# Unsplit weight halves in the mixers' projections and entry chunks, and another room for the experts' sixth chunk

## The chip, the cores and the metric

The kernel runs on one core of a Trainium2 chip. The metric is the time of one launch in microseconds of device time; it was taken in three runs. PE is TensorE (matmuls), PEld its weight loads, DVE is VectorE, ACT is ScalarE, POOL is GpSimd, SP is SyncE, whose queue issues all the transfers here.

## What is computed

A decoder trunk of two layers on 256 tokens of width 1024, in float32. Each layer: RMSNorm, an input projection whose 2304 columns feed four token mixers (a Conformer convolution, a pooling mixer, a dilated attention, a differential attention), an output projection, a residual add; then RMSNorm and a channel mixer, which is a dense SwiGLU in layer 0 and a choice of two of eight SwiGLU experts in layer 1.

```python
for layer in range(DEPTH):
    h = rms_norm(x, norm1_g[layer])
    x = x + token_mixing(h, w_in[layer], ...)      # 9 groups of 256 columns in, 1024 out
    h = rms_norm(x, norm2_g[layer])
    if layer % 2 == 0:
        x = x + swiglu(h, ffn_w_gate[i], ffn_w_up[i], ffn_w_down[i])    # 2816 wide
    else:
        x = x + moe_swiglu(h, moe_router[i], moe_w_gate[i], moe_w_up[i], moe_w_down[i])  # 8 x 3584 wide
return rms_norm(x, final_g)
```

## The kernel before

All weights lie in memory as one stream of chunks, 128 partitions by 2048 float32 columns, 1 MB each: 13 for each mixer, 33 for the dense channel mixer, 42 for each expert. `chunk` loads one into the next buffer of a ring. Until the experts the ring is one pool of nine buffers (`RING`). Before the experts the ring is written anew: eight further buffers (`RING2`), each a pool of its own, take the room that the second mixer's tiles had, and stand in the order between the pool's first `RING - LATE` turns and its last `LATE`. With `LATE = 3` the experts' chunks take six buffers of the old pool, then the eight new ones, then three of the old pool. The DMA queue is in order: a load that waits for its buffer holds all that stand behind it.

Products keep float32 accuracy by a split. `halves` cuts a chunk into two halves of 1024 columns and each of them into a high part (a copy on ACT, rounded to the format fp32r, line 190) and a low part (chunk minus high part, on DVE, or on POOL for the halves named in `on_pool`, line 191). The four pools of high and low parts hold four halves (`HALVES`). The tokens are split in the same way into `hTh` and `hTl`. A product is then three fp32r matmuls: high by high, low by high, high by low (`moving` where the weights stream through the array, `still` where the tokens do; `products` issues them, line 219). Some small products (line 655, the scores, the 64-row experts) are single matmuls on unsplit float32.

A stage begins with `enter`: for each block of 128 tokens it adds the last products of the stage before to the residual x (`run`, `add`), normalizes (`normed`), turns the block with eight transposes (`turned`) and copies it out of PSUM as high and low parts (`evict_high` for block 0, whose low parts are put off, `evict_parts` for block 1). Then `first` multiplies the block with the stage's first chunk (`token_major`, 24 matmuls of 256 columns). The order on DVE and ACT is written out by hand there; `hold` makes the next four splits stand behind the last copies. There are three such entries: the first mixer, the dense channel mixer, the second mixer. The experts have one of their own, not touched.

In `mixer`, behind the entry and one chunk of the same kind (c0 + 1), three calls of `project` compute 512 columns each from two chunks (queries and keys of the differential attention, then values, then queries and keys of the dilated attention). A chunk has two halves, a half two blocks of 128 input rows, and each block is multiplied with both blocks of tokens: 12 matmuls of 512 columns a half. The second half's low part is made on POOL, but for one chunk of the six. Between the halves DVE is given three of the 62 taps of the convolution (`some_taps`, line 401), and the rotary embedding (lines 439 to 442), the score blocks (line 475) and the scaling of the probabilities (lines 530, 531) follow on DVE. The output projection (`out_proj`) comes last. Outside `enter` a planner orders each engine's instructions, by modelled times.

In the experts the first turn and four more have 64 rows and use unsplit float32; three have 128 rows and split their chunks.

Of the kernel before, what the change touches and what calls it, by code (L numbers as in the profile page):

```python
# [10 lines left out]
F32 = mybir.dt.float32  # L11
# [4 lines left out]
AF = mybir.ActivationFunctionType  # L16
# [25 lines left out]
BIG = 4096.0  # L42
RING = 9
RING2 = 8
LATE = 3
HALVES = 4
FIRST = 0
START = 12
ORDER = ((0, 1, 2), (0, 2, 1))
FILL = 6  # L50
BUSY = ((4, 6), (0, 2, 4, 6), 4, 3)
TAPS = 3
# [41 lines left out]
def trunk(ctx: ExitStack, tc: tile.TileContext, x_in, wst, cst, par_a, par_l, gains, out):  # L94
# [80 lines left out]
    gain0 = gain(0)  # L175
    nc.sync.dma_start(cs, cst)

    def halves(c, on_pool=(), between=lambda: None):

        r = chunk(c) if isinstance(c, int) else c  # L180
        res = []
        for j in range(2):
            w = r[:, j * 1024:(j + 1) * 1024]
            hi = hi_p.tile([P, 1024], F32R, name="hi")
            lo = lo_p.tile([P, 1024], F32R, name="lo")
            eng = nc.gpsimd if j in on_pool else nc.vector
            with ExitStack() as st:
                for ins in behind if split[0] >= FIRST else ():
                    st.enter_context(tc.issue_after(ins))
                nc.scalar.activation(hi, w, AF.Copy)  # L190
                eng.tensor_tensor(out=lo, in0=w, in1=hi.bitcast(F32), op=SUB)  # L191
            split[0] += 1
            if split[0] == HALVES:
                behind.clear()
            res.append((hi, lo))
            if j == 0:
                between()
        return res
# [8 lines left out]
    def moving(ps, xx, w):  # L207

        return (ps, xx[0], w[0]), (ps, xx[1], w[0]), (ps, xx[0], w[1])
# [5 lines left out]
    def products(items, start=False, stop=False):  # L215

        seq = [m for it in items for m in it]
        for n, (ps, lhs, rhs) in enumerate(seq):
            nc.tensor.matmul(ps, lhs, rhs, start=start and all(m[0] is not ps for m in seq[:n]),  # L219
                             stop=stop and all(m[0] is not ps for m in seq[n + 1:]))  # L220

    def cut(pair, *at):
        return tuple(w[at] for w in pair)

    def part(hi, lo, src, eng=nc.vector):
        a = nc.scalar.activation(hi, src, AF.Copy)
        return a, eng.tensor_tensor(out=lo, in0=src, in1=hi.bitcast(F32), op=SUB)
# [46 lines left out]
            w = tuple(h.rearrange("p (k c) -> p k c", k=4) for h in hs[j])  # L274
            products([still(ps, cut(w, ALL, k, col), cut(hTp, ALL, 4 * j + k)) for k in range(4)], j == 0, j == 1)

    def token_major(ps, hs, t, order):

        tt = slice(t * P, (t + 1) * P)
        for j in range(2):  # L280
            w = tuple(h.rearrange("p (k c) -> p k c", k=4) for h in hs[j])
            items = [moving(ps, cut(hTp, ALL, 4 * j + k, tt), cut(w, ALL, k)) for k in range(4)]
            products([[it[n] for it in items] for n in order], j == 0, j == 1)

    def turned_back(src):

        ps = tr.tile([P, NT, P], F32, name="tr")
# [20 lines left out]
    def enter(before, c, first):  # L308

        run, add, gb = before[:3] if before else (lambda t, some: None, lambda t: None, gain0)
        eng = mybir.EngineType
        lows = []

        def evict_high(ps, kk, tt):

            h = nc.scalar.activation(hTh[:, kk, tt], ps, AF.Copy)
            lows.append(lambda: nc.vector.tensor_tensor(out=hTl[:, kk, tt], in0=ps, in1=hTh[:, kk, tt].bitcast(F32), op=SUB))  # L320
            return h

        with tc.manual_schedule(engines={eng.Activation, eng.DVE} if before else {eng.Activation, eng.DVE, eng.PE}):
            run(0, range(4))
            add(0)
            normed(0, xs[:, 0], gb)
            if before:
                hs = halves(c, (1,))
                run(1, range(3))
                turned(0, evict_high)  # L330
                lows[0]()
            else:
                hs = halves(c, (0,), lambda: turned(0, evict_parts))
                busy(FILL)
            run(1, range(3, 4))
            add(1)
            for f in lows[1:]:
                f()
            normed(1, xs[:, 1], gb, eng=nc.scalar)
            first(0, hs)  # L340
            last = turned(1, evict_parts)
        hold(*last)
        first(1, hs)

    def mixer(layer, c0, before):
        lam_init = 0.8 - 0.6 * math.exp(-0.3 * layer)
        psA = []

        def first(t, hs):
            if t == 0:  # L350
                psA.append(acc.tile([P, NT, 2, P], F32, name="acc"))
            token_major(psA[0][:, t].rearrange("p a c -> p (a c)"), hs, t, ORDER[int(t > 0 or before is not None)])

        enter(before, c0, first)
        if before:
# [1 line left out]
        with ExitStack() as held:  # L357
# [51 lines left out]
            def project(c, hooks=()):  # L409

                hooks = iter(hooks)
                ps = [acc.tile([P, 512], F32, name="acc") for _ in range(NT)]
                for j in range(2):
                    hs = halves(c + j, () if c + j == c0 + 5 else (1,))
                    for q in range(2):
                        w = tuple(h.rearrange("p (k c) -> p k c", k=2) for h in hs[q])
                        products([moving(ps[t], cut(hTp, ALL, 4 * j + 2 * q + k, slice(t * P, (t + 1) * P)), cut(w, ALL, k))
                                  for k in range(2) for t in range(NT)], j + q == 0, j + q == 2)
                        for _ in range(2):
                            for f in next(hooks, ()):  # L420
                                f()
                            some_taps(TAPS)
                return ps
# [246 lines left out]
        gb = gain(2 * layer + 1)  # L670
        parts = [h for n in (2, 3) for h in halves(c0 + 9 + n, (1,))]
        if layer == 1:

            ring[:] = ring[:-LATE] + [ctx.enter_context(tc.tile_pool(name=f"raw{n}", bufs=1, reuse_waits="tile"))
                                      for n in range(RING2)] + ring[-LATE:]
            turn[0] = 0
        return *add_products([(cut(hTp, ALL, ORD[4 + n]), h) for n, h in enumerate(parts)], po), gb, held

    def dense_ffn(c0, before):
        ps0 = []  # L680

        def first(t, hs):
            if t == 0:
                ps0.append(sc.tile([P, NT, 2, P], F32, name="sc"))
            token_major(ps0[0][:, t].rearrange("p a c -> p (a c)"), hs, t, ORDER[1])

        enter(before, c0, first)
        held = ExitStack()
        wk = held.enter_context(tc.tile_pool(name="fw", bufs=2, reuse_waits="tile"))
        ng = NFB // 2  # L690
        po = []

        def down(g, parts):
            hs = halves(c0 + 3 * g + 2)
            for n, hp in enumerate(parts):
                products([moving(po[2 * t + hf], cut(hp, ALL, slice(t * P, (t + 1) * P)), cut(hs[n], ALL, cc))
                          for t in range(NT) for hf, cc in enumerate(HF)], g + n == 0)

        prev, last = [], []
        for g in range(ng):  # L700
            parts = []
            for n in range(2):
                if g + n == 0:
                    gate, up = (ps0[0][:, :, a] for a in range(2))
                else:
                    hs = halves(c0 + 3 * g + n)
                    ps = sc.tile([P, 2, S], F32, name="sc")
                    for ab in range(2):
                        channel_major(ps[:, ab], hs, ab)
                    gate, up = (ps[:, a].rearrange("p (t c) -> p t c", t=NT) for a in range(2))  # L710
                sg = wk.tile([P, NT, P], F32, name="sgf")
                nc.scalar.activation(sg, gate, AF.Silu)
                h = wk.tile([P, NT, P], F32, name="hf")
                nc.vector.tensor_mul(h, up, sg)
                hh = wk.tile([P, S], F32R, name="hh", bufs=4)
                hl = wk.tile([P, S], F32R, name="hl", bufs=4)
                parts.append((hh, hl))
                if g + n == 0:
                    h0 = h
                else:  # L720
                    part(hh, hl, h.rearrange("p t c -> p (t c)"))
                if g == 0 and n == 1:
                    part(*parts[0], turned_back(h0))
            if g == 1:
                po.extend(acc.tile([P, 512], F32, name="acc") for _ in range(4))
            if 0 < g < ng - 1:
                down(g - 1, prev)
            last = prev + parts
            prev = parts
        gb = gain(2)  # L730
        parts = [h for g in (ng - 2, ng - 1) for h in halves(c0 + 3 * g + 2)]
        return *add_products(list(zip(last, parts)), po), gb, held

    def moe(c0, before):
        with ExitStack() as st:
# [395 lines left out]
            with tc.If(most > S):  # L1131
# [5 lines left out]
                    nc.vector.tensor_sub(pos2[:, t], pos[:, t], off)  # L1137
                experts([Turn(MOE0 + e * ECH, pos2, comb, e, True) for e in range(NE)])

    done = mixer(0, 0, None)  # L1140
    done = dense_ffn(FFN0, done)
    done = mixer(1, L1_0, done)
# [130 lines left out]
```

## Time and profile before

| | us |
|---|---|
| median of 3 runs | 1259.69 |
| lowest and highest of them | 1259.45, 1261.0 |
| the profiled execution | 1259.51 |
| its span, first to last instruction | 1257.7 |
| busy in it: PE, DVE, ACT, POOL | 1196.7, 735.8, 591.5, 73.9 |
| moved by DMA | 421.98 MB |
| mean granted TensorE clock | 0.987 |

By stage, in us from the span's start: the first mixer to about 112, the dense channel mixer with its entry to about 303, the second mixer to about 421, the experts' routing to 436, the experts to 1243, the last norm to the end. A share of busy time is an average over stages with different limits, so the stages are read one by one.

### The profile page before, as it was taken

How to read it: one execution, taken by the hardware profiler on the slowest of the kernel's cores; microseconds unless marked ns; L12 is line 12 of the kernel's file. 1: busy time of each engine (PE TensorE's matmuls, PEld its weight loads, DVE VectorE, ACT ScalarE, POOL GpSimd, SP SyncE). 2: the span in 40 equal slices, each digit the busy share in tenths (PEclk: the TensorE clock that was granted, in tenths of full speed). 3: DMA queues.
4: the chain of work that ended last, by engine and by line, in shares of the span. 5: the costliest groups of instructions: out<-in, count | busy, mean ns of one | idle time of the engine just before them, and what ended most of it. 6: DMA issues, size and time to landing. Idle time of an engine off the chain costs nothing.

```text
span 1257.7 us, 16634 instructions
## 1 busy us (share of the span) xinstructions
PE 1196.7 (95%) x6154; PEld 790.3 (63%) x6154; DVE 735.8 (58%) x1118; ACT 591.5 (47%) x868; POOL 73.9 (6%) x45
## 2 busy tenths in 40 slices
PE   8789999999888999999999999999999999999975
PEld 6677899998767633588853368874338887333221
DVE  5996655556898521688861188883139887212112
ACT  5374544444556421577741277772137776122112
POOL 3313000000511100000000000000000000000000
PEclk8899999999999999999999999999999999999998
DMA  9532655554532999999999999999999999999995
GB/s 362 213 128 101 230 183 191 184 196 157 193 134 110 413 420 420 419 418 418 417 361 421 419 420 419 419 419 405 420 419 419 420 419 419 415 418 420 420 420 221
DMA packets 60139, 421.98 MB, mean 336 GB/s; under 512 B 6672, under 2 KB 6928, under 8 KB 10256
## 3 DMA queue, kind: packets, MB, share of 16 engines
q1 hardware_dynamic: 60048, 420.82, 83.0%
q8 instruction: 50, 0.82, 0.3%
q14 instruction: 41, 0.34, 0.1%
HBM read 419.75 MB, written 1.05 MB: 335 GB/s over the span
## 4 chain that ended last, share of the span: by engine, by line
PE 58%; DMA 6%; DVE 1%; ACT 1%; issue 0%; POOL 0%; POOLq 0%; ACTq 0%; SPq 0%; DVEq 0%
PE acc L219 19%; PE acc L1004 16%; PE sc L219 9%; PE sc L1051 8%; DMA raw<-wst 6%; PE tr L955 1%; PE tr L1022 1%; PE tr L1071 1%; PE tr L1028 1%; DVE lo L191 1%; PE tr L974 0%; PE tr L965 0%; ACT hi L190 0%; DVE x L1072 0%; DVE raw L915 0%
## 5 line engine op out<-in xcount | busy, mean ns | idle before, releaser
L191 DVE TENSOR_TENSOR lo<-raw,hi 128x1024 fp32r<-128x1024 f32 x351 | 419.9, 1239 | 114.7 <-ACT hi L190 109.9
L190 ACT ACTIVATE hi<-raw 128x1024 fp32r<-128x1024 f32 x370 | 374.0, 1054 | 134.6 <-PE acc L219 61.4
L1004 PE MATMUL acc<-raw,xt 128*64 128x512 f32 x1096 | 251.3, 597 | 5.9 <-DMA raw<-wst 5.6
L1014 DVE TENSOR_TENSOR xs<-xs,acc 64x512 f32<-64x512 f32 x70 | 48.3, 690 | 276.4 <-ACT xs L1013 276.3
L1013 ACT ACTIVATE xs<-acc 64x512 f32<-64x512 f32 x70 | 41.3, 590 | 272.5 <-PE acc L1004 272.5
L1004 PEld LDWEIGHTS acc<-raw,xt 128*64 128x64 f32 x1096 | 73.7, 136 | 150.0 <-issue 131.7
L219 PE MATMUL acc<-lo,xgh 128*128 128x512 f32 x336 | 134.4, 400 | 1.9 <-DVE lo L191 1.6
L219 PE MATMUL acc<-hi,xgh 128*128 128x512 f32 x336 | 132.8, 395 | 0.0
L219 PE MATMUL acc<-hi,xgl 128*128 128x512 f32 x336 | 132.8, 395 | 0.0
L1051 PE MATMUL sc<-raw,ht 128*64 128x512 f32 x552 | 126.3, 594 | 5.0 <-ACT xs L1013 2.6
L219 PE MATMUL sc<-hTh,hi 128*128 128x256 f32 x336 | 93.0, 277 | 0.0
L219 PE MATMUL sc<-hTl,hi 128*128 128x256 f32 x336 | 92.9, 277 | 0.0
L219 PE MATMUL sc<-hTh,lo 128*128 128x256 f32 x336 | 92.9, 276 | 0.0
L1051 PEld LDWEIGHTS sc<-raw,ht 128*64 128x64 f32 x552 | 39.2, 137 | 84.1 <-issue 77.3
L219 PE MATMUL acc<-lo,hTh 128*128 128x512 f32 (+1 forms) x192 | 69.2, 387 | 10.5 <-DVE lo L191 10.4
L219 PEld LDWEIGHTS acc<-lo,xgh 128*128 128x128 f32 x336 | 63.2, 188 | 21.3 <-DVE lo L191 6.4
L219 PEld LDWEIGHTS acc<-hi,xgl 128*128 128x128 f32 x336 | 63.2, 188 | 14.9
L219 PEld LDWEIGHTS acc<-hi,xgh 128*128 128x128 f32 x336 | 63.3, 188 | 14.1
L219 PE MATMUL acc<-hi,hTh 128*128 128x512 f32 (+1 forms) x192 | 70.5, 395 | 0.0
L219 PE MATMUL acc<-hi,hTl 128*128 128x512 f32 (+1 forms) x192 | 70.1, 385 | 0.2
L219 PE MATMUL sc<-hi,hmh 128*128 128x512 f32 x168 | 66.7, 397 | 0.0
L219 PE MATMUL sc<-hi,hml 128*128 128x512 f32 x168 | 66.3, 395 | 0.0
(273 smaller groups left out, 1557.4 us busy)
## 6 DMA issues: line engine op xcount, KB each, us to landing
raw<-wst SPq DMA_DIRECT2D x389, 1024.0 KB, 16.4
raw<-gains SPq DMA_DIRECT2D x4, 512.0 KB, 5.5
raw<-wst SPq DMA_DIRECT2D x4, 512.0 KB, 13.0
hi<-wst SPq DMA_DIRECT2D x4, 512.0 KB, 14.2
lo<-wst SPq DMA_DIRECT2D x4, 512.0 KB, 13.8
pl<-par_l SPq DMA_DIRECT2D x2, 803.5 KB, 9.2
out<-raw SPq DMA_DIRECT2D x4, 256.0 KB, 3.2
x<-x_in SPq DMA_DIRECT2D x2, 256.0 KB, 3.3
```

The source lines that it names most:

```text
L190: nc.scalar.activation(hi, w, AF.Copy)
L191: eng.tensor_tensor(out=lo, in0=w, in1=hi.bitcast(F32), op=SUB)
L219: nc.tensor.matmul(ps, lhs, rhs, start=start and all(m[0] is not ps for m in seq[:n]), stop=stop and all(m[0] is not ps for m in seq[n + 1:]))
L955: nc.tensor.matmul(pg[q].rearrange("p k c -> p (k c)"), OH[e][:, t], src[:, t, HF[q]], start=t + n == 0, stop=t + n == 2)
L1004: m = nc.tensor.matmul(ps[ROWS[k % 2]], XT[e][:, 4 * j + k], w[:, k % 2], start=j == 0 and k < 2, stop=j == 1 and k > 1)
L1013: nc.scalar.activation(dst[ROWS[0]], ps[ROWS[0]], AF.Copy)
L1014: nc.vector.tensor_add(dst[ROWS[0]], dst[ROWS[0]], ps[ROWS[1]])
L1022: nc.tensor.transpose(ps[:, n, :NARROW], hm[ROWS[0], n * P:(n + 1) * P], ident[ROWS[0], ROWS[0]])
L1028: nc.tensor.transpose(ps[:, n], hm[:, n * P:(n + 1) * P], ident)
L1051: m = nc.tensor.matmul(DP[e][hf][ROWS[n]], HT[i][:, 2 * j + n], half(r, n)[:, HF[hf]], start=s + j == 0, stop=s == NSLAB - 1 and j == 1)
L1071: nc.tensor.matmul(ps, OT[e][:, t], y, start=n == 0, stop=n == 1)
```

## The change

Three things are done at once.

In `project` the first half of each chunk is not split. `halves` gets an argument `whole`: halves named there are handed on as they are. Their product is one float32 matmul of the unsplit tokens with the unsplit half. The second half's low part is made on DVE in all six chunks; POOL has none of them any more.

In `enter` the first chunk is not split at all. The block of tokens is copied out of PSUM once more, unsplit, into a new tile `full` (8 KB a partition), and `products_of` multiplies it with the chunk, eight float32 matmuls of 256 columns in place of 24. Both blocks get the extra copy, on ACT, ahead of the high copy. The first block's two low copies are made after the second residual add. `token_major` goes.

`full` lives in a pool of its own, ahead of the mixers' tiles, and is closed before the experts' ring is made; one of the eight new buffers takes its room. With `LATE = 4` the experts' sixth chunk takes that buffer in place of one of the old pool, and a later one takes the old pool's.

```diff
-LATE = 3
+LATE = 4
@@ halves
-    def halves(c, on_pool=(), between=lambda: None):
+    def halves(c, on_pool=(), between=lambda: None, whole=()):
...
             w = r[:, j * 1024:(j + 1) * 1024]
+            if j in whole:
+                res.append((w,))
+                continue
             hi = hi_p.tile([P, 1024], F32R, name="hi")
@@ enter
         def evict_high(ps, kk, tt):
 
+            a = nc.scalar.activation(full[:, kk, tt], ps, AF.Copy)
             h = nc.scalar.activation(hTh[:, kk, tt], ps, AF.Copy)
             lows.append(lambda: nc.vector.tensor_tensor(out=hTl[:, kk, tt], in0=ps, in1=hTh[:, kk, tt].bitcast(F32), op=SUB))
-            return h
+            return a, h
+
+        def evict_all(ps, kk, tt):
+            a = nc.scalar.activation(full[:, kk, tt], ps, AF.Copy)
+            return a, *part(hTh[:, kk, tt], hTl[:, kk, tt], ps)
+
+        def products_of(t):
+            tt = slice(t * P, (t + 1) * P)
+            ps = first(t)
+            for k in range(KD):
+                nc.tensor.matmul(ps, full[:, k, tt], r[:, k * 256:(k + 1) * 256], start=k == 0, stop=k == KD - 1)
 
         with tc.manual_schedule(engines={eng.Activation, eng.DVE} if before else {eng.Activation, eng.DVE, eng.PE}):
             run(0, range(4))
             add(0)
             normed(0, xs[:, 0], gb)
+            r = chunk(c)
             if before:
-                hs = halves(c, (1,))
                 run(1, range(3))
                 turned(0, evict_high)
-                lows[0]()
             else:
-                hs = halves(c, (0,), lambda: turned(0, evict_parts))
+                turned(0, evict_all)
                 busy(FILL)
             run(1, range(3, 4))
             add(1)
-            for f in lows[1:]:
+            for f in lows:
                 f()
             normed(1, xs[:, 1], gb, eng=nc.scalar)
-            first(0, hs)
-            last = turned(1, evict_parts)
+            products_of(0)
+            last = turned(1, evict_all)
         hold(*last)
-        first(1, hs)
+        products_of(1)
@@ project
-                    hs = halves(c + j, () if c + j == c0 + 5 else (1,))
+                    hs = halves(c + j, whole=(0,))
                     for q in range(2):
                         w = tuple(h.rearrange("p (k c) -> p k c", k=2) for h in hs[q])
-                        products([moving(ps[t], cut(hTp, ALL, 4 * j + 2 * q + k, slice(t * P, (t + 1) * P)), cut(w, ALL, k))
-                                  for k in range(2) for t in range(NT)], j + q == 0, j + q == 2)
+                        at = [(4 * j + 2 * q + k, k, t, slice(t * P, (t + 1) * P)) for k in range(2) for t in range(NT)]
+                        if q == 0:
+                            products([[(ps[t], full[:, b, tt], w[0][:, k])] for b, k, t, tt in at], j == 0)
+                        else:
+                            products([moving(ps[t], cut(hTp, ALL, b, tt), cut(w, ALL, k)) for b, k, t, tt in at], False, j == 1)
@@ end of mixer, layer 1
+            full_only.close()
@@ before the stages
+    full_only = ExitStack()
+    full = full_only.enter_context(tc.tile_pool(name="hf", bufs=1, reuse_waits="tile")).tile([P, KD, S], F32, name="hTf")
```

## Rows read from the trace of the kernel before

**Rows 1.** The page, busy tenths and GB/s in 40 slices of 31.4 us.

```profile
DVE  5996655556898521688861188883139887212112
...
GB/s 362 213 128 101 230 183 191 184 196 157 193 134 110 413 420 420 419 418 418 417 361 421 419 420 419 419 419 405 420 419 419 420 419 419 415 418 420 420 420 221
```

**Rows 2.** Windows: us, busy (count) of PE, PEld, DVE, ACT, POOL; clock, DMA, GB/s.

```profile
26.00:52.00 26.00, 19.18 (x77) 15.34 (x76) 25.52 (x48) 8.35 (x11) 8.75 (x4) 0.80 0.74 296
42.00:52.00 10.00, 6.22 (x15) 4.87 (x16) 10.00 (x28) 1.06 (x1) 0.00 (x0) 0.50 0.36 120
52.00:78.00 26.00, 25.99 (x143) 20.49 (x141) 22.81 (x66) 17.78 (x42) 8.64 (x2) 1.00 0.41 148
...
326.00:349.00 23.00, 17.38 (x76) 13.52 (x75) 22.82 (x39) 9.23 (x12) 16.90 (x4) 1.00 0.32 115
349.00:385.00 36.00, 32.04 (x172) 25.82 (x172) 34.83 (x104) 20.36 (x49) 2.39 (x1) 0.91 0.39 147
```

**Rows 3.** Waits of PE, 26 to 112 us: total, times, longest.

```profile
PE acc L219 <- DVE lo L191: 6.8, 1, 6.8
```

**Rows 4.** Groups of DVE, 26 to 80 us: busy us, mean ns, idle before.

```profile
L401 DVE SCALAR_TENSOR_TENSOR cv<-zp,pl,cv 128x256 f32<-128x256 f32 x60 | 30.8, 581 | 0.0
L191 DVE TENSOR_TENSOR lo<-raw,hi 128x1024 fp32r<-128x1024 f32 x9 | 11.1, 1252 | 1.7 <-ACT hi L190 1.7
...
L475 DVE CUSTOM_DVE_ANT_0 pD<-sc,pl 128x128 f32<-128x128 f32 x8 | 1.9, 284 | 3.0 <-PE sc L469 3.0
```

**Rows 5.** Timeline of DVE, 326 to 350 us: start, us, instruction.

```profile
327.03 2.33 DVE L399 TENSOR_SCALAR cv<-zp,pl 128x256 f32<-128x256 f32 x1 [0.18 <-ACT zp L390]
...
338.26 1.21 DVE L191 TENSOR_TENSOR lo<-raw,hi 128x1024 fp32r<-128x1024 f32 x1
339.39 2.62 DVE L401 SCALAR_TENSOR_TENSOR cv<-zp,pl,cv 128x256 f32<-128x256 f32 x1
341.93 2.50 DVE L439 TENSOR_TENSOR xc<-xs,pl 128x128 f32<-128x128 f32 x1
...
344.56 0.47 DVE L401 SCALAR_TENSOR_TENSOR cv<-zp,pl,cv 128x256 f32<-128x256 f32 x1
...
345.62 0.28 DVE L439 TENSOR_TENSOR xc<-xs,pl 128x128 f32<-128x128 f32 x1
...
346.03 2.56 DVE L401 SCALAR_TENSOR_TENSOR cv<-zp,pl,cv 128x256 f32<-128x256 f32 x1
```

**Rows 6.** Timeline of POOL, 300 to 412 us.

```profile
345.62 2.69 POOL L191 TENSOR_TENSOR lo<-raw,hi 128x1024 fp32r<-128x1024 f32 x1 [1.33 <-ACT hi L190]
```

**Rows 7.** Chain of work that ended last: start, us, what, how many.

```profile
408.87 1.74 PE sc L655 x8
...
549.56 11.14 PE acc L219 x48
```

**Rows 8.** Timeline of ACT, 305 to 323 us.

```profile
316.54 1.26 ACT L226 ACTIVATE hTh<-tr 128x512 fp32r<-128x512 f32 x2 [2.48 <-PE tr L263]
317.70 2.95 ACT L190 ACTIVATE hi<-raw 128x1024 fp32r<-128x1024 f32 x3
```

**Rows 9.** Timeline of DVE, 305 to 327 us.

```profile
308.06 3.43 DVE L191 TENSOR_TENSOR lo<-raw,hi 128x1024 fp32r<-128x1024 f32 x1
...
318.78 3.50 DVE L191 TENSOR_TENSOR lo<-raw,hi 128x1024 fp32r<-128x1024 f32 x3 [0.25 <-ACT hi L190]
```

**Rows 10.** Waits of the DMA queue, 378 to 413 us.

```profile
SPq L159 <- DVE lo L191: 27.6, 2, 22.5
SPq L159 <- PE sc L666: 5.5, 1, 5.5
```

**Rows 11.** Windows in the experts, columns as in rows 2.

```profile
644.00:655.00 11.00, 11.00 (x49) 3.83 (x49) 4.91 (x7) 2.90 (x5) 0.00 (x0) 1.00 0.87 329
655.00:860.00 205.00, 203.50 (x924) 127.41 (x920) 127.31 (x134) 109.40 (x136) 0.00 (x0) 1.00 1.01 419
```

**Rows 12.** Waits of the DMA queue, 641 to 655 us.

```profile
SPq L159 <- PE acc L1004: 8.7, 4, 3.1
```

More of the change, by code (lines that the diff above doesn't have):

```diff
@@ L48 @@
 START = 12
-ORDER = ((0, 1, 2), (0, 2, 1))
 FILL = 6
@@ L275, in channel_major @@
             products([still(ps, cut(w, ALL, k, col), cut(hTp, ALL, 4 * j + k)) for k in range(4)], j == 0, j == 1)
[L277 to L283, printed above, removed]
     def turned_back(src):
@@ L347, in mixer, with first @@
         psA = []
-        def first(t, hs):
+        def first(t):
             if t == 0:
                 psA.append(acc.tile([P, NT, 2, P], F32, name="acc"))
-            token_major(psA[0][:, t].rearrange("p a c -> p (a c)"), hs, t, ORDER[int(t > 0 or before is not None)])
+            return psA[0][:, t].rearrange("p a c -> p (a c)")
         enter(before, c0, first)
@@ L680, in dense_ffn, with first @@
         ps0 = []
-        def first(t, hs):
+        def first(t):
             if t == 0:
                 ps0.append(sc.tile([P, NT, 2, P], F32, name="sc"))
-            token_major(ps0[0][:, t].rearrange("p a c -> p (a c)"), hs, t, ORDER[1])
+            return ps0[0][:, t].rearrange("p a c -> p (a c)")
         enter(before, c0, first)
```

## The prediction

> **What bounds the kernel now.** I read the slices of the page first [rows 1]. From about 400 us to the end the transfers run at 418 to 420 GB/s with two dents (361 and 405), so the experts stream their weights at the pace of memory. Before 400 us they run at 100 to 230 GB/s: memory has room there, and something on the core sets the time. The table by stage [rows 2] says what. In the two mixers' wide projections VectorE (DVE) is the fullest engine: 25.52 of 26.00 us in one stretch of mixer 0, 22.82 of 23.00 and 34.83 of 36.00 in mixer 1, while TensorE (PE) does 19.18, 17.38 and 32.04. The waits of PE [rows 3] agree: its longest wait in mixer 0, 6.8 us, is for a low half made by DVE, and behind it PE runs at a granted clock of 0.50 (1.2 of its two levels, 1.2 and 2.4 GHz) for ten us [rows 2]. Only 52 to 78 us is full on PE (25.99 of 26.00). So a saving on DVE in the mixers moves the start of the experts.
>
> Does an earlier start of the experts move the end? At 644 to 655 us the stream drops to 329 GB/s [rows 11] while the DMA queue waits 8.7 us for PE's reads of earlier chunks [rows 12]: all buffers were full and PE, in its first 128-row expert, was behind. PE's path from the start of the experts up to there is therefore on the chain, and behind it the stream runs full. If PE starts X earlier, that point comes X earlier and so does the end, as long as the stream is not the later one; it had 31.4 us x (1 - 361/419) = 4.4 us to spare in that slice [rows 1, 11], and its own start moves too (below). I pass X on whole.
>
> **Projections, DVE.** Each mixer has six wide chunks of two halves. Before, the first half's low part is made on DVE (1.21 us, [rows 5]) and, in five chunks of six, the second's on GpSimd (Pool). After, first halves have no low part and second halves' are made on DVE. So DVE loses six lows and gains five: -1.2 us a mixer. The larger part is what Pool does to DVE. While a Pool split runs (345.62 for 2.69 us, [rows 6]) a DVE tap that starts at 346.03 takes 2.56 us; alone it takes 0.47 [rows 5]. The same holds for 327.03 (2.33), 339.39 (2.62) and 341.93 (2.50 where the like operation takes 0.28). In mixer 1 that is (2.33 + 2.62 + 2.50 + 2.56) - (0.47 + 0.47 + 0.28 + 0.47) = 8.3 us, all under Pool splits that the change takes away. In mixer 0 the grouped rows give it: 60 taps of 581 ns where 470 is normal [rows 5], 6.6 us [rows 4]. The one Pool split of the output projection stays, with its 2 us. Mixer 0 also has 3.0 us in which DVE sat idle for score products that PE had not reached [rows 4], because PE had lost 6.8 us and then its clock; PE no longer waits for a low part in the first half of each chunk, and with one pair of buffers a chunk in place of two the splits can run two chunks further ahead. I count the 3.0 as gone. Sum: mixer 0 6.6 + 1.2 + 3.0 = 10.8, mixer 1 8.3 + 1.2 = 9.5.
>
> **Projections, PE.** A split product is three matmuls of 512 columns; 48 take 11.14 us [rows 7], 0.232 each, 0.70 a product. A 128x128 float32 matmul of 512 columns is not in this trace. The nearest row is line 655, float32, 128x128 weights, 256 columns: eight in 1.74 us [rows 7], 0.217 each, so I take 0.434 at 512. Bounds: 0.217 (as if the width cost nothing) and 0.70 (no gain). By 0.434 a half costs 4 x 0.434 = 1.74 in place of 2.79, -1.05, six times: -6.3 us of PE a mixer, which keeps PE ahead of DVE and is not added to the sum; at 0.70 PE would just stay where it is, and of the sum only the 3.0 idle would come back.
>
> Here a rule of the Trainium skill speaks against the change. "FP8 and Floating Point Precision", section TensorE Precision Notes, gives true FP32 four passes through the array. By it a 512-column product would take four times a one-pass 0.232, 0.93 against the 0.70 of the split one, and PE would gain work. Line 655's row is against it: 0.217 is about twice, not four times, what 256 columns take in one pass at half of 0.232.
>
> **Entries.** Three entries (mixer 0, dense FFN, mixer 1) follow one pattern. Removed: two high parts on ACT, a low part on DVE and one on Pool. At mixer 1 that DVE low takes 3.43 us [rows 9] since it collides with Pool's, and it stands ahead of the second residual add. Added: for each 128 tokens two plain ACT copies from PSUM. At the second block they stand between its two high copies (1.26 us for a pair, [rows 8]) and the next chunk's high parts (from 317.70, [rows 8]), whose low parts (from 318.78, [rows 9]) the next products need; the hold on the last evictions keeps that order, and ACT's queue behind it holds nothing but these. Cost +1.26 us each. Return: the add can start when PE's last products allow, about 1 us sooner, but the two held-back low copies now follow it ahead of the norm's scalar; I take, as an estimate, 1.0 back at FFN and mixer 1, and 0.1 at mixer 0, whose second block waits for its load. Together +1.2 + 0.3 + 0.3 = +1.8 us, bounds 0 to 3.8. The entry products themselves shrink from three matmuls to one of 0.217 and need ACT's copy alone, but the next chunk's split is late next, so I cost them at nothing; if ACT's order let the split go first, they would give up to 1 us each.
>
> **The sixth chunk.** Its DMA stands behind a wait of 22.5 of the 27.6 us for a split of the output projection [rows 10], in an idle memory stretch, and the queue is in order, so all later ones stand behind it. With the room of the unsplit tokens (last read in the third projection) it and the next few can go some 20 us sooner. But the stream then meets the next wait, for the last attention product (5.5 us, [rows 10]), which isn't moved: the chunks already taken are 2.5 us each (1 MB at 419 GB/s, [rows 11]), and between them and that wait the queue idles again; I estimate that one chunk's 2.5 us is left of it. That makes the stream earlier, not PE, so at 644 us the buffers are full again a little sooner: 0. Without this edit, the room would cost nothing either.
>
> **Sum.** 10.8 + 9.5 - 1.8 = 18.5 us. DVE is an in-order queue and won't be full all the time: PE, now with less work, waits longer before the last score blocks, and a wait of 6.8 us cost it ten us at half clock with 6.22 busy, 3.1 lost [rows 2, 3]. I charge 1.75 a mixer: -15. The profiled execution took 1259.5 (span 1257.7, 1.8 around it), the median of the runs is 1259.7: forecast 1245.
>
> **The rivals.**
> 1. DVE's queue gives bubbles: taps are queued ahead of the lows that PE needs, as is the case now at PE's wait of 6.8 us [rows 3], so only half of the saved time shows. For it: the order is made from modelled times and PE waits on DVE in other places too. Against: two fewer buffers per chunk. -4 to -10, 1253.
> 2. Slower: the six extra copies on ACT at the entries lie on the path and the mixers return nothing, because DVE's freed time is only waited out. Price 3 x 1.26 = 3.8, 1263. It decides once the mixers give back less than 1.9 us each; the 8.3 us of measured stalls speak against it.
> 3. The stream takes it: if loads of experts cannot start sooner, everything before is only waiting; 1257 to 1261. Against: every room they wait for is freed by mixer 1 itself.
> 4. A float32 matmul of 512 columns takes four passes of 0.232 [rows 7], 0.93: per mixer 24 x (0.93 - 0.70) = +5.5 us on PE in place of -6.3. PE then needs as long as DVE, the 3.0 idle stays and by estimate 2 us a mixer are lost to PE: 18.5 - 3.5 - 3.0 - 4 = 8, 1252. This is the skill's rule, above; line 655 is against it.
> 5. All of it comes, with the experts' early loads and no clock loss: -18 to -22, 1239.
>
> **Chances.** Forecast (-10 to -18) 0.56, rival 1 0.20, rival 2 0.06, rival 3 0.06, rival 4 0.04, rival 5 0.08. Bounds of the unknown costs (entries 0 to 3.8, idle 3.0, clock 0 to 6) keep the forecast within 1241 to 1250; the range for 8 in 10 takes in most of rivals 1, 4 and 5: 1238 to 1255. A measurement tells about 0.2% (2.5 us). Faster 0.88, within 0.06, slower 0.06.
>
> **What would show it.** After: Pool has no split between the entry and the output projection; no tap in the mixers over 0.5 us but one; mixer 1's projections end some 10 us sooner relative to its entry; float32 matmuls of 512 columns 0.43 apart; ACT with four copies in a row at each entry's second block; the dent at 640 us still there, a little deeper. The forecast is wrong if DVE in the mixers stands idle by more than 5 us each, if PE's clock is at 0.50 for over 15 us there, or if the dent vanishes and the stream runs at 419 GB/s from its start.

## The result, and the profile after

The changed kernel takes 1246.8 us (median of four runs, 1244.4 to 1250.7) against 1260.35 beside it: a ratio of 0.9899, 95% interval 0.9876 to 0.9922. The forecast was 1245, range 1238 to 1255. The total came as forecast; two of its steps have the wrong sign (PE's price for a float32 product, and the entries), and the runs below show what stood in for them.

The profiled execution is one of 1248.1 us. Its page, engines and slices, the counterpart of [rows 1]:

```profile
PE 1203.4 (97%) x6058; PEld 781.3 (63%) x6058; DVE 709.4 (57%) x1113; ACT 578.1 (46%) x862; POOL 30.7 (2%) x32
...
DVE  4975655555985512888841298883148886212112
...
GB/s 363 245 102 102 238 203 190 168 200 165 184 203 172 411 419 420 419 419 420 395 373 419 419 419 420 419 420 404 419 420 418 420 419 417 417 419 419 419 420 208
```

DVE's busy time fell by 26.4 us and Pool's by 43.2. The experts start 12.3 us earlier (first gather at 419.7 us, before at 432.0), and the dent in the stream spreads over two slices (395 and 373 GB/s, where one had 361). The windows are the counterpart of [rows 2], with the same columns:

```profile
26.00:52.00 26.00, 26.00 (x101) 16.59 (x101) 24.69 (x62) 7.67 (x11) 0.00 (x0) 1.00 0.74 294
52.00:78.00 26.00, 25.35 (x143) 17.75 (x143) 22.11 (x77) 16.40 (x45) 2.40 (x1) 1.00 0.57 203
82.70:92.90 10.20, 10.06 (x41) 8.78 (x41) 7.09 (x31) 5.01 (x16) 2.08 (x2) 0.50 0.00 0
...
322.00:349.00 27.00, 27.00 (x92) 16.48 (x91) 27.00 (x71) 8.43 (x11) 0.00 (x0) 1.00 0.37 137
349.00:385.00 36.00, 31.96 (x194) 23.41 (x193) 29.84 (x115) 21.67 (x66) 4.48 (x3) 1.00 0.62 230
```

From 26 to 52 us PE was busy 19.18 us; now it is busy 26.00, and in mixer 0 DVE is the one with time to spare. In mixer 1 (322 to 349 us) both are full, 27.00 of 27; e9 and e10 below tell which of them sets the time. The half clock at 42 to 52 us is gone, and another has come at 82.7, in the mixer's tail. PE's waits from 26 to 112 us, for [rows 3]:

```profile
PE sc L476 <- DVE nm L482: 1.6, 1, 1.6
PE tr L458 <- DVE xs L449: 0.7, 1, 0.7
```

No wait of PE for a low part is left. DVE's groups, 26 to 80 us, for [rows 4] (the last column is DVE's idle time before them and what ended it):

```profile
L405 DVE SCALAR_TENSOR_TENSOR cv<-zp,pl,cv 128x256 f32<-128x256 f32 x60 | 24.6, 480 | 0.0
L193 DVE TENSOR_TENSOR lo<-raw,hi 128x1024 fp32r<-128x1024 f32 x10 | 12.1, 1223 | 0.5 <-ACT hi L192 0.5
L482 DVE CUSTOM_DVE_ANT_0 pD<-sc,pl 128x256 f32<-128x256 f32 x8 | 3.0, 418 | 1.9 <-PE sc L476 1.9
L446 DVE TENSOR_TENSOR xc<-xs,pl 128x128 f32<-128x128 f32 x4 | 2.7, 686 | 1.6 <-ACT xs L438 1.6
```

The 60 taps fell from 30.8 to 24.6 us, 480 ns each in place of 581. And PE's groups from 26 to 70 us, the costliest:

```profile
L221 PE MATMUL acc<-raw,hTf 128*128 128x512 f32 x48 | 21.7, 594 | 0.0
L221 PE MATMUL acc<-hi,hTh 128*128 128x512 f32 x24 | 11.2, 467 | 0.0
L221 PE MATMUL acc<-lo,hTh 128*128 128x512 f32 x24 | 9.4, 394 | 0.0
L221 PE MATMUL acc<-hi,hTl 128*128 128x512 f32 x24 | 9.4, 391 | 0.0
```

This is the row that the prediction had wrong. The code issues four products per half, 24 in the six unsplit halves and 24 in the six split ones. The split ones show 24 rows for each of their three matmuls; the unsplit ones show 48. **A float32 matmul leaves two rows.** On the timeline of PE:

```profile
28.09 3.60 PE L221 MATMUL acc<-raw,hTf 128*128 128x512 f32 x8
...
34.29 3.60 PE L221 MATMUL acc<-raw,hTf 128*128 128x512 f32 x8
```

Eight rows for four products, 3.60 us from the first start to the last end, with the last row's own 0.594 in it: the starts are 0.429 us apart ((3.60 - 0.594) / 7). So a float32 product of 512 columns takes 0.858 us, more than the three split matmuls (0.70).

### The profile page after: what moved, and what is told of

It reads as the page before. It is cut to its first block, busy times and chain, and to the rows that moved or that the text cites. A ratio compares the mean times of both kernels' runs of the same rounds, so it can differ in the third digit from the quotient of the medians.

```text
span 1246.1 us, 16416 instructions
## 1 busy us (share of the span) xinstructions
PE 1203.4 (97%) x6058; PEld 781.3 (63%) x6058; DVE 709.4 (57%) x1113; ACT 578.1 (46%) x862; POOL 30.7 (2%) x32
## 4 chain that ended last, share of the span: by engine, by line
PE 52%; DMA 14%; DVE 1%; ACT 1%; issue 0%; POOL 0%; POOLq 0%; SPq 0%; ACTq 0%; DVEq 0%
PE acc L221 19%; DMA raw<-wst 14%; PE acc L1012 13%; PE sc L221 9%; PE sc L1059 6%; PE tr L963 1%; PE tr L1036 1%; PE tr L1079 1%; PE tr L1030 1%; DVE lo L193 1%; ACT hi L192 0%; DVE x L1080 0%; PE tr L973 0%; DVE raw L923 0%; PE tr L982 0%
## 5 line engine op out<-in xcount | busy, mean ns | idle before, releaser
L193 DVE TENSOR_TENSOR lo<-raw,hi 128x1024 fp32r<-128x1024 f32 x346 | 406.9, 1220 | 115.8 <-ACT hi L192 112.7
L192 ACT ACTIVATE hi<-raw 128x1024 fp32r<-128x1024 f32 x352 | 355.0, 1055 | 109.3 <-PE acc L221 48.5
L221 PEld LDWEIGHTS sc<-hTl,hi 128*128 128x128 f32 x336 | 63.2, 188 | 0.4
L221 PEld LDWEIGHTS sc<-hTh,hi 128*128 128x128 f32 x336 | 63.1, 188 | 0.4
L221 PEld LDWEIGHTS sc<-hTh,lo 128*128 128x128 f32 x336 | 63.1, 188 | 0.0
```

## Experiments

To place a saving I cut each profiled execution at the same events: the first tap of a mixer, the last scaling of the first attention's weights (between them lie the wide projections), the last attention product, the first gather of the experts, and the end. In us, from the timelines (each time is that of the profiled execution, one per kernel):

| kernel | first tap to scaling, mixer 0 / 1 | from there to the last attention product, 0 / 1 | gather to end |
|---|---|---|---|
| before | 57.2 / 57.6 | 27.7 / 28.3 | 825.7 |
| after | 50.9 / 49.2 | 30.6 / 28.4 | 826.4 |
| e1, five early | 50.9 / 49.2 | 29.7 / 28.4 | 826.3 |
| e2, entries alone | 58.7 / 57.7 | 28.8 / 29.6 | 827.0 |
| e3, FFN's entry split | 50.9 / 49.2 | 30.6 / 30.3 | 827.4 |
| e4, lows on Pool | 56.0 / 54.3 | 29.6 / 30.4 | 825.8 |
| e5, before, lows on DVE | 54.4 / 53.2 | 29.4 / 27.4 | 826.2 |
| e9, fewer taps | 50.9 / 49.2 | 29.6 / 28.4 | 826.0 |
| e10, half the products | 46.9 / 44.6 | 30.0 / 29.3 | 826.2 |
| e11, all split on DVE | 54.8 / 51.6 | 29.3 / 28.9 | 826.7 |
| e12, three unsplit | 49.2 / 47.9 | 27.7 / 27.7 | 825.6 |

**e1: the sixth early chunk undone.**

```diff
-LATE = 4
+LATE = 3
```

> The changed kernel with the sixth early chunk undone (five loads of the experts before mixer 1 ends, as before the change), all else kept. Theory (the prediction's step): the stream of the experts starts about one chunk, 2.5 us, later, but at about 640 us all buffers are full and PE's path decides, so the time stays that of the changed kernel, 1246.8 within 1.5 us; the dent in the stream at 600 to 660 us gets smaller by about 2.5 us of stream. Rival (the earlier chunk counts in full, the stream decides): 1249.3. Rival (the room costs, and undoing it gains): under 1245.

Measured: 1248.2 (1245.7 to 1249.5), ratio 0.9901 (0.9886 to 0.9916); after has 0.9899. No difference, as the theory has it. The last column of the table says why: from the first gather to the end it is 826.3 against 826.4, whichever stream started first. The dent's windows, first e1, then after:

```profile
600.00:660.00 60.00, 59.91 (x275) 33.80 (x275) 33.22 (x38) 25.72 (x35) 0.00 (x0) 1.00 0.96 384
```

```profile
600.00:660.00 60.00, 59.91 (x274) 34.90 (x274) 33.93 (x38) 26.32 (x36) 0.00 (x0) 1.00 0.96 382
```

384 against 382 GB/s is 60 x 2/419 = 0.3 us of stream, not the 2.5 expected of the dent. That the chunk is worth nothing is shown; that the dent swallows it is not.

**e2: the unsplit entries alone** (`project` as before the change).

```diff
-                    hs = halves(c + j, whole=(0,))
+                    hs = halves(c + j, () if c + j == c0 + 5 else (1,))
...
```

> The changed kernel with the mixers' wide projections split as before the change (both halves, the second's low part on Pool), the unsplit entries and the sixth chunk kept. Theory as the two traces now suggest: the entries gained about 3 us (FFN 2, mixer 1 one), so the projections carry 10: 1257 (1255 to 1258.5). The prediction's own terms: the entries lose 1.8, so 1262. Rival (the entries carry most): 1250 or less.

Measured: 1259.9 (1258.9 to 1262.8), ratio 0.9996 (0.9988 to 1.0005): outside the theory's range, between the two. The way from mixer 0's last attention product to mixer 1's first tap, with two entries in it, is 211.4 us against 213.8 before, so they did bring 2.3. The mixers of the profiled run, the slowest of the twelve (1262.8), are 1.5 and 0.2 longer up to the scaling and 1.1 and 1.3 behind it, with the clock at half in six short stretches of them (before has three). In the total, the entries alone are worth nothing that can be measured.

**e3: the dense FFN's entry alone as before** (`enter_split` is the former `enter`, with `token_major`).

```diff
...
-        enter(before, c0, first)
+        enter_split(before, c0, first)
```

> The changed kernel with the dense FFN's entry alone as before the change (split chunk, three products per block, second half's or first half's low on Pool, no plain copies). Theory from the traces: the unsplit FFN entry is worth about 2.0 us, so 1248.8 (1248 to 1250). The prediction's terms: the unsplit entry costs 1.26 and returns 1.0, so undoing it gives 1246.5 (0.3 sooner). Rival (ACT's two more copies are on the path in full and nothing returns): 1245.5.

Measured: 1249.5 (1248.4 to 1251.6), ratio 0.9909 (0.9897 to 0.9922), 0.0010 or 1.3 us over after, within both intervals, and as the theory had it (1248 to 1250). The trace is plainer: from mixer 0's last attention product to the FFN's first activation it takes 21.4 us here and before, 20.2 after and in e2, e4 and e11. The unsplit entry gains 1.2 us. Mixer 1's entry on ACT, after, shows the price and what stands behind:

```profile
310.59 0.60 ACT L319 ACTIVATE hTf<-tr 128x512 f32<-128x512 f32 x1 [2.79 <-PE tr L265]
311.09 0.59 ACT L228 ACTIVATE hTh<-tr 128x512 fp32r<-128x512 f32 x1
311.56 0.60 ACT L319 ACTIVATE hTf<-tr 128x512 f32<-128x512 f32 x1
312.04 0.62 ACT L228 ACTIVATE hTh<-tr 128x512 fp32r<-128x512 f32 x1
312.52 2.98 ACT L192 ACTIVATE hi<-raw 128x1024 fp32r<-128x1024 f32 x3
```

Four copies in a row, and the next chunk's high parts 1.93 us after the first. Before, with a pair, they came 1.16 after it (316.54 to 317.70, [rows 8]): two more copies cost 0.77 (FFN, 1.17 to 1.92: 126.89 to 128.06 in e3, 125.69 to 127.61 after), while in the FFN's entry the second block's first copy comes 2.0 sooner after the mixer's end.

**e4: the second halves' lows back on Pool** (first halves stay unsplit).

```diff
-                    hs = halves(c + j, whole=(0,))
+                    hs = halves(c + j, () if c + j == c0 + 5 else (1,), whole=(0,))
```

> The changed kernel with the second halves' low parts of the wide projections back on Pool (five of six in a mixer); first halves stay unsplit. Theory (Pool's splits hold DVE up): each Pool split of about 2.7 us stalls a DVE operation by about 2 us, so per mixer DVE loses 5 x 1.21 = 6.05 us of work and gains 5 x 2.05 = 10.3 of stalls, +4.2; PE has idle cover for about half of it: 1250 (1248 to 1254), and taps of over 2 us show again. Rival (the stalls cost nothing, the lows' own work was the load): 6 us a mixer come free on DVE and the time falls, 1243 or less, or stays within 1.5 us of 1246.8 if PE is the bound by now.

Measured: 1255.9 (1254.3 to 1257.1), ratio 0.9961 (0.9948 to 0.9973): 7.8 us over after by the ratios, 9.1 by the medians; 5.1 in each mixer up to the scaling. More than the 1250 (to 1254) expected, and by another way than DVE's sum: its stalls (60 taps 28.5 us in place of 24.6, one of the two first taps 2.56 in place of 0.41) come to about what the five lows cost (6.05). But a stall stands where it hurts: the taps are ahead of the rotary steps in DVE's queue, and PE waits for those. DVE's taps, 26 to 80 us, and PE's waits, 26 to 92 us (0.7 after, in place of the 3.4):

```profile
L405 DVE SCALAR_TENSOR_TENSOR cv<-zp,pl,cv 128x256 f32<-128x256 f32 x60 | 28.5, 551 | 0.0
...
PE tr L458 <- DVE xs L449: 3.4, 3, 2.4
PE sc L476 <- DVE nm L482: 1.6, 1, 1.6
```

**e5: the kernel before, with only the lows moved off Pool.**

```diff
-                    hs = halves(c + j, () if c + j == c0 + 5 else (1,))
+                    hs = halves(c + j, ())
```

> The kernel before with one thing changed: all low parts of the mixers' wide projections on DVE, none on Pool; nothing is unsplit. Theory (the stalls under Pool's splits cost DVE 6.6 and 8.3 us a mixer, its own five more lows cost 6.05): DVE comes out 0.5 and 2.3 us ahead, so 1257.5 (1255.5 to 1259). Rival (leaving Pool is the whole of the gain, since e4 lost 9 us by going back): 1250 or less. Rival (the stalls hit only work that had time): 6 us a mixer more on DVE, 1266 to 1272.

Measured: 1251.75 (1250.8 to 1253.8), ratio 0.9940 (0.9926 to 0.9953). Nothing is unsplit here, and more than half of the change's gain is there; the theory's 1257.5 was missed by 6. DVE's groups, 26 to 80 us:

```profile
L401 DVE SCALAR_TENSOR_TENSOR cv<-zp,pl,cv 128x256 f32<-128x256 f32 x60 | 24.6, 481 | 0.0
L191 DVE TENSOR_TENSOR lo<-raw,hi 128x1024 fp32r<-128x1024 f32 x13 | 15.5, 1217 | 0.6 <-ACT hi L190 0.6
```

The taps lose 6.2 us against [rows 4], as the prediction had it from the stalls (6.6). The mixers gain 2.9 and 4.3, two more each than DVE's sum gives. PE's waits show where they can come from. In mixer 0 its wait for low parts is 3.7 us in place of 6.8 [rows 3], and of the ten us at half clock behind it 3.4 are left there (54.4 to 57.8; the tail has 6.8 of its own, from 88.5):

```profile
PE acc L219 <- DVE lo L191: 3.7, 3, 1.6
```

In mixer 1 (320 to 412 us) the kernel before had this wait for the rotary step, and e5 has none:

```profile
PE tr L451 <- DVE xs L442: 3.8, 2, 2.9
```

A rival would be that PE waited for Pool's slow low parts themselves. It didn't: no wait of PE in either mixer of the kernel before is put down to Pool.

**e6: PE kept busy in the tails.**

```diff
                 for g in range(2):
                     scores(qkC, pC, lC, 2, g, i, 64.0 ** -0.5, R_MC)
+                if i == 0:
+                    pTD = transposed(pD, 4, 2)
+                    busy(6, cs.bitcast(BF16)[:, :P], cs.bitcast(BF16)[:, :512])
...
-            pTD = transposed(pD, 4, 2)
```

> The changed kernel with six idle bf16 matmuls of 512 columns on PE in each mixer's tail, in the wait of 1.6 us before the second block's scores (the transposes of the first attention's weights are called ahead of those scores, so that the fillers stand in that wait). They compute nothing that is used. Theory (the granted clock at 0.50 behind that wait costs the tail 1 to 3 us, and its coming and going makes the runs spread from 1244.4 to 1250.7): no stretch at 0.50 in the mixers' tails, 1244.5 (1243 to 1246), and a spread of less than 3 us. Rival (PE waits there for DVE anyway, the clock costs nothing): 1247 with the same spread, or 1 to 2 us later by the fillers' own time.

Measured: 1249.5 (1246.4 to 1250.8), ratio 0.9921 (0.9907 to 0.9935). Not what the theory said. In the profiled execution mixer 0 had no half clock and its tail was 29.75 us in place of 30.6, but mixer 1 had one at 375 to 382, where after has none, and the tail's order moved with the edit. In mixer 1 the six matmuls did not keep the clock up. What a tail without a dip is worth isn't settled by this run, but e3 settles it for mixer 1 (below, under the clock).

**e7 and e8: the 128-row experts unsplit too**, e8 with five early chunks.

```diff
-                            hs = halves(r)
...
+                            for k in range(4):
+                                w = half(r, k // 2).rearrange("p (k c) -> p k c", k=2)
+                                nc.tensor.matmul(ps, XT[e][:, 4 * j + k], w[:, k % 2], start=j + k == 0, stop=j == 1 and k == 3)
...
```

> The changed kernel with the three 128-row experts unsplit too: their tokens are evicted once as float32 and multiplied with the chunks as they land, one float32 matmul of 512 columns in place of three; no split of their weights. Theory (at 600 to 660 us PE is behind with the three matmuls per product, 2.79 us a chunk against 2.49 us of stream, which is why the sixth chunk and the earlier stream are worth nothing): PE needs 1.74 us a chunk, the dent goes, the stream runs full from its start to its end: the 5 us lost at 600 to 660, and 1 to 2 elsewhere, come back: 1240 (1237 to 1243). Rival (the dent comes from the buffers' order, or a chunk that is held until PE has read it keeps its buffer longer): 1247 or later.

> As e7, with the sixth early chunk undone. Theory (with PE no longer behind, the stream decides from its start): the chunk is worth its 2.5 us here, so 2.5 later than e7, while it was worth 0 in the changed kernel. Rival (its load is followed by a wait that takes back what it gained, wherever PE stands): the time of e7.

Measured: 1321.9 (ratio 1.0496, 1.0482 to 1.0511) and 1320.9 (1.0487, 1.0472 to 1.0501). Both missed what was expected (1240, and 2.5 later), because a float32 product was priced at one row there. The stream at 600 to 700 us in e7, to about 655 in a 128-row expert:

```profile
600.00:700.00 100.00, 100.00 (x354) 40.88 (x354) 14.51 (x22) 14.20 (x26) 0.00 (x0) 1.00 0.88 336
```

PE is full, and while such an expert runs the loads go out 3.43 us apart, now and then 3.87: four products of 0.858 are 3.43. Three matmuls took 4 x 0.70 = 2.79. Over 3 x 42 chunks that is 126 x (3.43 - 2.79) = 81 us; the runs show 75. So PE decides there, more than before, and e8 can't tell what the sixth chunk would be worth to a PE with time; it stays open.

**e9: less work on DVE.**

```diff
-            taps = [(ct, k) for k in range(CW) for ct in range(2)]
+            taps = [(ct, k) for k in range(CW - 10) for ct in range(2)]
```

> The changed kernel with 20 of the 62 convolution taps of each mixer left out (the last ten of each half; that part of the convolution isn't computed): 20 x 0.48 = 9.6 us less work on DVE a mixer. Theory (a float32 product of 512 columns is two records 0.429 apart, 0.86, so the unsplit halves cost PE 3.9 us more a mixer, and PE, busy 26.00 of 26 us at 26 to 52, is the bound now): little comes back, 1243 to 1247. Rival (DVE still sets the mixers' time, as before the change): 8 us or more a mixer, 1231 or less.

Measured: 1246.7 (1245.4 to 1250.9), ratio 0.9907 (0.9889 to 0.9925). 9.6 us a mixer off DVE, and nothing moves: the table has the same 50.9 and 49.2. Its windows:

```profile
26.00:52.00 26.00, 26.00 (x96) 16.39 (x95) 23.96 (x57) 7.67 (x11) 0.00 (x0) 1.00 0.75 302
52.00:78.00 26.00, 25.34 (x147) 17.71 (x145) 15.21 (x63) 17.57 (x47) 2.40 (x1) 1.00 0.54 197
322.00:349.00 27.00, 27.00 (x100) 16.75 (x99) 22.03 (x59) 9.06 (x14) 0.00 (x0) 1.00 0.45 157
```

DVE falls to 15.21 in mixer 0 (22.11 after) and to 22.03 in mixer 1 (27.00 after); PE stays as full. After the change DVE no longer sets the mixers' time.

**e10: less work on PE.**

```diff
-                            products([[(ps[t], full[:, b, tt], w[0][:, k])] for b, k, t, tt in at], j == 0)
+                            products([[(ps[t], full[:, b, tt], w[0][:, k])] for b, k, t, tt in at if k == 0], j == 0)
```

> The changed kernel with half of the unsplit products of the wide projections left out (the second of the two 128-row blocks of each unsplit half isn't multiplied): 6 x 2 x 0.858 = 10.3 us less on PE a mixer, the same work on DVE and ACT. Theory (PE is the bound now, DVE close behind it at 24.69 of 26): 2 to 4 us a mixer come back until DVE stops it, 1239 to 1243. Rival (DVE is the bound): 1246 to 1247. Rival (PE alone sets the time): 1227.

Measured: 1238.85 (1237.5 to 1239.4), ratio 0.9835 (0.9819 to 0.9851). Of 10.3 us a mixer 4.0 and 4.6 come back; then DVE is the fuller (25.41 of 26 us at 26 to 52, PE 24.48), and each mixer has 6.8 us at half clock (from 63.9 and 350.6), which after hasn't there. With e9 this shows PE as the bound, and DVE some 4 us behind or a little more, as the half clock's part of it isn't known. The window of mixer 0:

```profile
26.00:52.00 26.00, 24.48 (x100) 16.22 (x99) 25.41 (x67) 12.01 (x19) 0.00 (x0) 1.00 0.85 338
```

**e11 and e12: how many halves to leave unsplit.** e11 splits all on DVE; e12 leaves the first chunk's first half of each projection unsplit, three in place of six.

```diff
-                    hs = halves(c + j, whole=(0,))
+                    hs = halves(c + j, whole=(0,) if j == 0 else ())
...
-                        if q == 0:
+                        if len(w) == 1:
...
```

> The changed kernel with the first halves of the wide projections split as well, all low parts on DVE; entries unsplit as in the change. DVE does 6 x 1.21 = 7.3 us more a mixer, PE 6 x 0.64 = 3.9 less. Theory (with the lows off Pool, DVE is the bound in this form and the unsplit halves are worth the rest): as e5 less what the unsplit entries bring, 1250.5 (1249 to 1252). Rival (the entries bring 3 us beside e5): 1248.5. Rival (PE's price of the unsplit halves outweighs them): 1246 or less, and the unsplit halves were a loss.

> The changed kernel with three of the six unsplit halves of each mixer split again on DVE (the second chunk of each projection): DVE 3.6 us more a mixer, PE 1.9 less. Theory (PE is full and DVE nearly so): the best split lies between, 1246 (1244.5 to 1248). Rival (DVE has no room at all): halfway to e11, 1248.5 or later.

Measured: e11 1251.0 (1249.8 to 1253.9), ratio 0.9929 (0.9915 to 0.9943); e12 **1239.95** (1239.0 to 1242.9), ratio **0.9853** (0.9833 to 0.9872), faster than both kernels. Windows of e12:

```profile
26.00:52.00 26.00, 26.00 (x101) 18.14 (x100) 25.76 (x63) 11.03 (x16) 0.00 (x0) 1.00 0.84 334
52.00:78.00 26.00, 24.94 (x153) 18.47 (x151) 25.25 (x91) 18.34 (x53) 2.93 (x1) 1.00 0.47 163
322.00:349.00 27.00, 26.92 (x116) 18.64 (x115) 27.00 (x76) 13.88 (x29) 0.00 (x0) 1.00 0.34 117
349.00:385.00 36.00, 31.81 (x198) 25.30 (x197) 32.88 (x110) 24.13 (x58) 9.81 (x7) 1.00 0.55 205
```

PE and DVE are both full. PE's 1.9 us less a mixer come through as 1.7 and 1.3 up to the scaling. Behind it no wait of PE is over 0.6 us up to 112, the granted clock is 1.00 in both mixers, and the tails are 2.9 and 0.7 shorter than after's. The theory had 1246 (1244.5 to 1248) for the balance and nothing for the clock. Of the 6 us between the kernels about two are the clock of e12's runs (mean 0.992 to 0.997): at 0.996 it takes 1239.7 and 1240.2, and after 1244.4. In e11 DVE has 7.3 us more work than in after and PE 3.9 less, and it is 4 us slower; PE waits for DVE's low parts again, 3.7 us in mixer 0 as in e5. There DVE is the bound, as the theory had it (1250.5).

## Why the prediction was right, step by step

**The bound and the pass-through: right.** DVE set the mixers' time before (e5 and e11 bear it out), and what the mixers save arrives whole: gather to end is 825.6 to 827.4 in all eleven executions of the table. Rival 3 (the stream takes it) is out.

**Pool's stalls on DVE: right in mechanism and size** (6.2 measured for 6.6 in mixer 0), and e4 and e5 show them to be the greater part: moving the lows alone gives 7.7 of the 13.5 us. Net of the five lows' own work I expected 0.5 and 2.3 us of e5; 2.9 and 4.3 came. PE's shorter waits behind the queue are the likely rest: e4 has such waits and e5 has lost them, but no run parts them from DVE's own time.

**The 3.0 us of idle and mixer 0's sum: too high.** Forecast 10.8, measured 6.3 up to the scaling; mixer 1 9.5 and 8.4. Step "Projections, PE" failed, and with it the 3.0: DVE still idles 1.9 us for the score products of 256 columns, 1.6 before the rotary step (the groups L482 and L446 above). I had read eight rows of line 655 [rows 7] as eight matmuls; its loops (two by two) issue four. So 256 columns cost 0.434 and 512 cost 0.858, not 0.434; PE didn't gain 6.3 us a mixer but lost 6 x 4 x (0.858 - 0.70) = 3.8. The sign that the prediction named, float32 rows 0.43 apart, did come (0.429) and says nothing by itself: each such row is half a product.

The prediction also called line 655 the nearest row. A nearer one stood on the page of the kernel before, float32 products of 512 columns in the 64-row experts (128x64 weights):

```profile
L1004 PE MATMUL acc<-raw,xt 128*64 128x512 f32 x1096 | 251.3, 597 | 5.9 <-DMA raw<-wst 5.6
```

Five experts with 28 such chunks of four products make 560 products, so this row too has about two records for each. On the timeline at 703 to 705 us two products run side by side, one for each half of the output's rows; 12 records, six pairs, take 2.74 us, the last of them 0.592, so the pairs start 0.43 us apart ((2.74 - 0.592) / 5). The count and the price, 0.858, could have been read before the change.

The dearer product is the condition of rival 4, at 0.86 in place of its 0.93. Its time (1252) did not come: it carried the entries' loss of 1.8, and took off 7 us for PE and the idle time, where the mixers fell short of the forecast by 4.5 and 1.1 (10.8 - 6.3, 9.5 - 8.4). PE holds the mixers up only by as much as its load is over DVE's (e9, e10). The entry's products were dearer than priced, too: 16 rows 0.215 us apart for eight products, 3.4 us, where the 24 before (0.118 apart) took 2.8. The rule of the Trainium skill that I set aside ("FP8 and Floating Point Precision", TensorE Precision Notes: true FP32 takes four passes) comes near these traces: the estimate by it was 0.93, from fp32r matmuls of 512 columns that start 0.232 apart, and 0.858 was measured.

**Entries: wrong by sign.** Forecast +1.8 in all. The FFN's gained 1.2 where I had lost 0.3 (return 2.0 for 1.0, price 0.75 for 1.26). Mixer 1's gained about as much: with both, the way between the mixers is 2.3 shorter in e2 than before (211.4 for 213.8), and 2.5 in e11 than in e5 (212.5 for 215.0), where all lows are on DVE. In after it is only 1.2 shorter (212.6), since its lows are on DVE as well, and mixer 1's first tap comes 1.2 later by that (e4, with lows on Pool, has 211.4). So the entries brought about 2.3 us, and 1.2 of mixer 1's 8.4 is taken back ahead of its first tap.

**The sixth chunk: 0, right** (e1). Why it is 0 is shown only as far as the time behind the gather doesn't depend on it.

**The clock: 3.5 charged, and something like it came, in another place.** I put it into bubbles before the score blocks; it came in mixer 0's tail, 2.9 us longer than before, with ten us at 0.50 behind a wait of 1.6 us, as [rows 2, 3] show ten behind a wait of 6.8. It differs from run to run: in e1, the same program up to there, the half clock lasts 3.4 us in place of 10.2 and that tail is 0.9 us shorter. What ten such us cost can be read in mixer 1, where e3 and after run the same instructions in the same order on PE, with the same wait of 1.6 us: e3 has 10.2 us at 0.50 there (375.5 to 385.7), after none, and e3's tail is 1.9 us longer (30.3 for 28.4). By that, as an estimate, 1.9 of mixer 0's 2.9 is the clock and about one the tail's changed order, the wait in it; no run shows that tail of after without the half clock. e12's tail, at full clock, has the 27.7 of before.

Net, in the profiled pair: projections -14.7, tails +2.9, entries with the start -0.7, experts +0.7, together -11.7 of span (1257.7 to 1246.1). The forecast's -15 was -20.3 for the mixers, +1.8 for the entries and +3.5 for the clock. That the mixers' shortfall of 5.6 was partly made up by the entries, and that the range had room for the rest, was luck: with PE out of the way (e10) 1239 was there, and e12 has nearly all of it by splitting three halves again.

## What to carry to other kernels

Count rows against the instructions that the loops issue before taking a price per instruction: two rows a matmul turned a cost into a gain here, and three expectations that rested on it (the PE term, e7, e8) fell together. When a change takes work from the fullest engine and gives it to the next one, ask how far it can go before the second is the bound, and try the amount between: six unsplit halves gave 1.0%, none 0.7%, three 1.5%. An engine that stalls another through a shared resource costs more than its share of busy time, since the stall stands in the queue ahead of what a third engine waits for.

## What the runs showed of the hardware that was not expected

A float32 matmul is two rows in the profile, and a 512-column one costs 0.858 us against 0.70 for the three matmuls of a split product: splitting is cheaper on PE at this shape. A DVE operation with two SBUF inputs that starts while a Pool split of 2.4 to 2.7 us runs lasts until the split's end (0.47 becomes 2.62, [rows 5]). A Pool split can wait for DVE in its turn: before the change one that started at 54.49, amid taps one behind the other, took 6.24 us. The Trainium skill's "SBUF — State Buffer" (SBUF: two separate sides) has this as an exclusive lock on a port pair that the two share, and the traces agree. And the runs' times go with the granted clock: over the nine runs of after and e1, whose mixers are the same, mean clock 0.985 to 0.996 goes with 1250.7 to 1244.4 us, a straight line of 0.57 us for each 0.001. The line alone doesn't show which of the two moves the other, but the pair of tails above does for one stretch: the same instructions, 1.9 us more with ten us at half clock. So a change of 2 us is read from stretches of the traces rather than from medians.
